# Column sums as rounded parts, a layer norm with a fixed place in the weight stream, and a rotation by transfers

## The chip, the cores and the metric

The kernel runs on one core of a Trainium2 chip. The metric is the device time of one execution in microseconds (us). A core has a matrix engine (TensorE, PE in the profile), a vector engine (VectorE, DVE), a scalar engine with function tables (ScalarE, ACT), a general engine (GpSimd, POOL), a queue engine (SyncE, SP), and DMA engines. Each engine takes its own instructions in a fixed order, and engines wait for each other by semaphores.

## The reference, cut to what matters

Two decoder layers run over 512 prompt tokens and 8 sample tokens (520 columns here), 1024 channels wide:

```python
def hybrid_layer(x, ...):
    h = rms_norm(x, norm_g)
    glu, gate_a, q, k, v, gate_b, mg_a, mg_b = split_in(h @ w_in)
    u = glu[..., :CONV_WIDTH] * sigmoid(glu[..., CONV_WIDTH:])
    c = depthwise_conv31(concat([conv_buf, u])) + conv_b
    c = silu(layer_norm(c, ln_g, ln_b)) * silu(gate_a)
    y_a = c @ w_conv_out
    q, k = partial_rope(q, pos), partial_rope(k, pos)   # 16 of 64 dims: x1*cos - x2*sin, x2*cos + x1*sin
    o = windowed_attention_with_sinks(q, k, v)
    y_b = (o * silu(gate_b)) @ w_attn_out
    return x + (sigmoid(mg_a) * y_a + sigmoid(mg_b) * y_b) @ w_out
```

A final rms_norm follows the second layer. All is float32, to a tolerance that plain bfloat16 products would miss.

## The kernel before, in words

Channels lie on the 128 partitions and tokens run along a row, so an activation of 1024 channels is eight tiles of 128x520. The weights of a layer come as 82 **units** of 1024x128: one DMA from SP brings a unit (`raw`, two buffers), ACT rounds it to fp32r (`whi`, L126), DVE subtracts to get the rest (`wlo`, L127; three buffers each). `Unit.step` (L134) issues three matmuls for each of eight channel tiles and each half of 260 tokens: high times high, low times high, high times low. That is 48 matmuls a unit. Activations are split the same way (`split`: ACT cast L97, DVE subtraction L98). A unit's two result banks (`mm`) are double-buffered, so a unit can't begin until the work that reads the result of the unit two before it is done; the third GLU unit of a layer uses two spare banks, `T` and `V`.

The order in a layer is: GLU 16 units in pairs a and b (i = 0 to 7), K, V, Q 8, gate_b 8, MB and MA 16 (between which stand the attention's scores L506, transposes L532 and values L541), gate_a 8, YB 8, YA 8, OUT 8. Below, gate_a 1 is the first unit of gate_a, and so on. The first three GLU pairs multiply rows that aren't normalized yet; the factor R of the rms norm (`rstd`: ACT Ln and Exp L183 and L186, DVE L184 to L189) is multiplied into their results, and the normalized rows `hh, hl` are made meanwhile (DVE L266, cast L97, subtraction L98) for the fourth pair onward. A scheduler sets the order on each engine, with priorities and `issue_after` ties from the program.

A sum over channels (`Sum`) adds eight tiles on DVE (L165) and then multiplies the float32 total `ssum` with a matrix of ones on PE, one matmul for each half (`total`, L170). This happens for the rms norm of each layer, for the mean and the variance of the convolution's layer norm (L600 on), and at the end. The layer norm then scales eight tiles (L613) on DVE, and YB's units end in `mgb = result * mgb` (L641), which frees the unit's banks. Results of gate_a are copied out by ACT (L620). ACT also makes 24 sigmoids of gate values (L623, L624, L626), tied behind the last Exp of the attention. K's rotation takes the partner rows by two float32 matmuls with a permutation matrix (L348), read out of PSUM by two multiplications (L349).

Of the kernel before, what the change touches and what calls it, by code (L numbers as in the profile page):

```python
# [10 lines left out]
F32R = mybir.dt.float32r  # L11
AF = mybir.ActivationFunctionType
ALU = mybir.AluOpType

D = 1024
# [4 lines left out]
HALF = TOK // 2  # L20
KT = 8
TAPS = 31
PAD = TAPS - 1
HD = 64
# [8 lines left out]
W_GLU, W_K, W_V, W_Q, W_GB, W_MB, W_MA, W_GA, W_YB, W_YA, W_OUT = (  # L33
    0, 16, 17, 18, 26, 34, 42, 50, 58, 66, 74)
# [2 lines left out]
P_G, P_CW, P_CB, P_LG, P_LB, P_SK, P_SS = 0, 8, 256, 264, 272, 280, 296  # L37
N_P = 297

C_ID, C_SW, C_MASK, C_FG = 0, 128, 256, 512  # L40
N_C = 520


@with_exitstack
def hybrid_step(ctx, tc, x_in, w_in, par, const, rope, conv_st, kc_in, vc_in,
                y_out, ncp, nkp, nvp, ncs, nks, nvs):
    nc = tc.nc
# [21 lines left out]
    def g(dt=F32):  # L69
        return gp.tile([128, TOK], dt, tag="g", name=name("g"))  # L70
# [4 lines left out]
    def two(t):  # L75
        return t.rearrange("p (a b) -> p a b", a=2)

    def sbank():
        return psS.tile([128, 512], F32, tag="S", name=name("S"))
# [6 lines left out]

    con = cst.tile([128, N_C], F32, name="con")
    ident = con[:, C_ID:C_ID + 128]
    swap = con[:, C_SW:C_SW + 128]
    ones = cst.tile([128, 128], F32, name="ones")  # L90
    V.memset(ones, 1.0)
    eps = cst.tile([128, 1], F32, name="eps")
    V.memset(eps, EPS)

# [52 lines left out]
    class Sum:  # L147
# [27 lines left out]
        def totals(self):  # L175
            return [self.total(0), self.total(1)]

    def rstd(sums, halves=(0, 1)):
        y0, v, a = tmp("y0", 1), tmp("v", 1), tmp("a", 1)
        c = slice(halves[0] * HALF, (halves[-1] + 1) * HALF)  # L180
        for hf, s in zip(halves, sums):
            h = slice(hf * HALF, (hf + 1) * HALF)
            A.activation(y0[:, h], s, AF.Ln, bias=eps, scale=1.0 / D)  # L183
            V.tensor_scalar(v[:, h], s, 1.0 / D, EPS, op0=ALU.mult, op1=ALU.add)  # L184
        y0, v, a = y0[:, c], v[:, c], a[:, c]
        A.activation(y0, y0, AF.Exp, scale=-0.5)  # L186
        V.scalar_tensor_tensor(a, y0, -0.5, y0, op0=ALU.mult, op1=ALU.mult)
        V.tensor_tensor(v, v, a, op=ALU.mult)
        V.scalar_tensor_tensor(v, v, 1.5, y0, op0=ALU.add, op1=ALU.mult)  # L189
        return v  # L190
# [4 lines left out]
    def square(x):  # L195
        s = tmp("sq", 3)
        A.activation(s, x, AF.Square)
        return s
# [49 lines left out]
        after(rows, xt[i], i)  # L248
    after(squares)
    nc.sync.dma_start(con, const)  # L250
    xres = None

    for l in range(L):
# [20 lines left out]
        for i in range(KT):  # L274
# [6 lines left out]
            if i == 0:  # L281
                for k in range(KT):
                    for u in first:
                        u.step(0, k)
                        u.step(1, k)
                R = rstd(sq.totals())
                a, b = first
            else:
                a = Unit(l, W_GLU + 2 * i, *src, spare=(i == 1))
                a.half(0)  # L290
                a.half(1)
            u = up.tile([128, PAD + TOK], F32, tag="u", name=f"u{l}_{i}")
# [40 lines left out]


        kps = Unit(l, W_K, hh, hl).both()
        kn, kcos, ksin, krot = g(), g(), g(), g()
        nc.gpsimd.dma_start(kcos, rope[2])
        nc.gpsimd.dma_start(ksin, rope[3])
        A.copy(two(kn), kps)
        V.tensor_tensor(krot, kn, kcos, op=ALU.mult)  # L340
        vps = Unit(l, W_V, hh, hl).both()
        vt = g()
        A.copy(two(vt), vps)
        nc.gpsimd.dma_start(nvp[l], vt[:, T - 128:T])
        for hf in range(2):
            c = slice(hf * HALF, (hf + 1) * HALF)
            kss = sbank()
            PE.matmul(kss[:, :HALF], swap, kn[:, c], start=True, stop=True)  # L348
            V.tensor_tensor(ksin[:, c], kss[:, :HALF], ksin[:, c], op=ALU.mult)  # L349
        V.tensor_tensor(krot, krot, ksin, op=ALU.add)  # L350
        nc.gpsimd.dma_start(nkp[l], krot[:, T - 128:T])
        KH, KL = [], []
        for kv in range(2):
# [248 lines left out]
        for i, c in enumerate(cs):  # L602
            sm.add(i, c)
        mu = tmp("a", 1)
        for hf, s in enumerate(sm.totals()):
            A.mul(two(mu)[:, hf, :], s, -1.0 / D)
        sm = Sum()
        for i, c in enumerate(cs):
            V.tensor_tensor(c, c, mu, op=ALU.add)
            sm.add(i, square(c))  # L610
        R2 = rstd(sm.totals())
        for c in cs:
            V.tensor_tensor(c, c, R2, op=ALU.mult)  # L613


        sga = []
        for i in range(KT):
            ps = Unit(l, W_GA + i, hh, hl).both()
            s = g()
            A.copy(two(s), ps)  # L620
            sga.append(s)
            with tc.issue_after(exp_ins[0].ins):
                A.activation(mgb[i], mgb[i], AF.Sigmoid)  # L623
                A.activation(mga[i], mga[i], AF.Sigmoid)  # L624
                sg = tmp("sq", 3)
                A.activation(sg, s, AF.Sigmoid)  # L626
            V.tensor_tensor(s, s, sg, op=ALU.mult)
# [15 lines left out]

        yh, yl = [], []
        for i in range(KT):
            ps = Unit(l, W_YA + i, ch, cl).both()
            V.tensor_tensor(two(mga[i]), ps, two(mga[i]), op=ALU.mult)  # L647
            V.tensor_tensor(mga[i], mga[i], mgb[i], op=ALU.add)
            a, b = split(mga[i], new=og)
            yh.append(a)  # L650
            yl.append(b)
# [93 lines left out]
def _constants():  # L745
# [2 lines left out]
    r = np.arange(128)  # L748
    con[r, C_ID + r] = 1
    d = r % HD  # L750
    partner = np.where(d < 8, r + 8, np.where(d < 16, r - 8, r))
    con[r, C_SW + partner] = 1
    j = np.arange(256)[None, :]
    q = r[:, None]
    ok = np.where(j < 128, j > q, j - 128 <= q)
# [74 lines left out]
```

## Time and profile before

| what | value |
|---|---|
| time, median of 3 runs | 1064.87 us (1064.74 to 1064.91) |
| profiled execution, its own time | 1064.98 us |
| its span, first to last instruction | 1063.2 us |
| mean granted clock of TensorE | 0.997 |
| busy PE, DVE, ACT, POOL | 99%, 80%, 49%, 7% |

The span is 1.8 us shorter than the execution's own time. PE's busy share is that of a pipeline: a matmul is shown with some 284 ns, while the next one starts about 0.12 us after it. So lengths are read from starts: in the second layer's third GLU unit 47 matmuls lie between the starts 541.88 and 547.52 us, 0.12 us each, and a unit takes 5.76 us.

### The profile page before, as it was taken

To read this page: it belongs to the slowest core of one execution; us is meant where nothing else is said; L and a number is where in the kernel's file an instruction comes from. 1 tells how busy PE (TensorE), PEld (TensorE's weight loads), DVE (VectorE), ACT (ScalarE), POOL (GpSimd) and SP (SyncE) were. 2 spreads that over 40 slices of the span, in tenths; PEclk is the share of its full clock that TensorE was granted. 3 is DMA by queue.
4 is the path that set the end of the run, shared out by engine and by line. 5 is a ranking of instruction groups with operands and counts; after the bars stand their busy time and mean duration, and the time that the engine had idled before them with its cause. 6 is when DMAs were issued, how large, how long until landed. Compare 5 with 4: busy or idle time off the path is not lost.

```text
span 1063.2 us, 21526 instructions
## 1 busy us (share of the span) xinstructions
PE 1049.8 (99%) x8742; PEld 1034.9 (97%) x8742; DVE 855.4 (80%) x1572; ACT 516.5 (49%) x953; POOL 79.5 (7%) x180
## 2 busy tenths in 40 slices
PE   8999999999999999999999999999999999999996
PEld 8999999999999999999999999999999999999995
DVE  7999999999999587455569999899999976944545
ACT  7621433356667784224453234434576686822322
POOL 0001211001011000000101013100001000000000
PEclk9999999999999999999999999999999999999998
DMA  7334574332321215233334337633232212252312
GB/s 234 127 120 132 173 237 144 102 117 80 105 90 66 80 60 198 82 100 117 133 100 140 120 113 238 205 119 119 81 112 81 87 60 80 87 178 95 99 61 81
DMA packets 45220, 126.42 MB, mean 119 GB/s; under 512 B 6384, under 2 KB 10048, under 8 KB 45120
## 3 DMA queue, kind: packets, MB, share of 16 engines
q1 hardware_dynamic: 39024, 111.81, 32.0%
q0 software_dynamic: 4800, 12.16, 3.6%
q8 instruction: 68, 1.11, 0.4%
q10 hardware_dynamic: 1296, 1.07, 0.3%
q14 instruction: 32, 0.26, 0.1%
HBM read 107.66 MB, written 17.36 MB: 118 GB/s over the span
## 4 chain that ended last, share of the span: by engine, by line
PE 97%; DVE 1%; DMA 1%; SPq 0%; issue 0%; ACT 0%; DVEq 0%; ACTq 0%
PE mm L134 86%; PE S L506 3%; PE pv L541 3%; PE PT L532 2%; PE T L134 1%; PE S L170 1%; PE V L134 1%; DMA g<-x 1%; DMA raw<-w 0%; DVE g L696 0%; DVE ssum L165 0%; PE S L464 0%; PE pvs L486 0%; SPq L123 0%; PE S L348 0%
## 5 line engine op out<-in xcount | busy, mean ns | idle before, releaser
L134 PE MATMUL mm<-g,whi 128*128 128x260 f32 x4160 | 766.2, 284 | 1.0 <-ACT g L215 1.0
L134 PEld LDWEIGHTS mm<-g,whi 128*128 128x128 f32 x4160 | 644.8, 188 | 2.0 <-ACT g L215 1.2
L134 PE MATMUL mm<-g,wlo 128*128 128x260 f32 x2080 | 588.9, 283 | 0.0
L134 PEld LDWEIGHTS mm<-g,wlo 128*128 128x128 f32 x2080 | 392.0, 188 | 0.1
L595 DVE SCALAR_TENSOR_TENSOR acc<-u,par,acc 128x512 f32<-128x512 f32 x464 | 329.0, 744 | 0.2
L126 ACT CAST whi<-raw 128x1024 fp32r<-128x1024 f32 (+1 forms) x168 | 172.9, 1029 | 205.9 <-PE mm L134 165.1
L127 DVE TENSOR_TENSOR wlo<-raw,whi 128x1024 fp32r<-128x1024 f32 (+1 forms) x168 | 200.8, 1196 | 52.7 <-ACT whi L126 52.4
L134 PE MATMUL mm<-o,whi 128*128 128x260 f32 x992 | 179.3, 282 | 1.0 <-DVE g L685 1.0
L134 PEld LDWEIGHTS mm<-o,whi 128*128 128x128 f32 x992 | 153.1, 188 | 1.5 <-issue 0.8
L134 PE MATMUL mm<-o,wlo 128*128 128x260 f32 x496 | 139.5, 282 | 0.0
L134 PEld LDWEIGHTS mm<-o,wlo 128*128 128x128 f32 x496 | 93.2, 188 | 0.0
L518 ACT ACTIVATE p<-p,sm 128x257 f32<-128x257 f32 (+1 forms) x128 | 60.9, 479 | 18.7 <-DVE sm L512 18.6
L512 DVE CUSTOM_DVE_ANT_0 p<-S,con,nsk 128x256 f32<-128x256 f32 (+1 forms) x128 | 52.8, 447 | 7.9 <-PE PT L532 6.1
L534 ACT COPY pts<-PT 128x256 f32<-128x256 f32 (+1 forms) x64 | 33.7, 526 | 50.2 <-PE PT L532 50.2
L510 POOL COPY p<-nsk 128x2 f32<-128x2 f32 x64 | 26.0, 413 | 342.9 <-PE PT L532 289.0
L647 DVE TENSOR_TENSOR g<-mm,g 128x520 f32<-128x520 f32 x16 | 11.2, 700 | 43.1 <-PE mm L134 43.1
L506 PE MATMUL S<-g,g 128*128 128x256 f32 x256 | 41.6, 283 | 0.0
L445 ACT ACTIVATE g<-mm 128x520 f32<-128x520 f32 x16 | 9.7, 606 | 56.7 <-PE mm L134 56.7
L532 PE MATMUL PT<-con,p 128*128 128x128 f32 x224 | 35.6, 276 | 0.0
L506 PEld LDWEIGHTS S<-g,g 128*128 128x128 f32 x256 | 35.1, 188 | 0.0
L641 DVE TENSOR_TENSOR g<-mm,g 128x520 f32<-128x520 f32 x16 | 11.1, 695 | 28.8 <-PE mm L134 28.8
L522 ACT ACTIVATE p<-p,sm 128x128 f32<-128x128 f32 (+1 forms) x64 | 30.5, 480 | 7.5 <-DVE sm L521 7.3
(168 smaller groups left out, 817.5 us busy)
## 6 DMA issues: line engine op xcount, KB each, us to landing
raw<-w SPq DMA_DIRECT2D x162, 512.0 KB, 3.4
qscr<-g SPq DMA_DIRECT2D x32, 256.0 KB, 4.3
g<-qscr SPq DMA_DIRECT2D x32, 256.0 KB, 3.8
g<-x SPq DMA_DIRECT2D x16, 260.0 KB, 4.9
g<-rope POOLq DMA_DIRECT2D x8, 260.0 KB, 4.6
xres<-g POOLq DMA_DIRECT2D x8, 260.0 KB, 2.3
g<-xres SPq DMA_DIRECT2D x8, 260.0 KB, 4.9
ncs<-g POOLq DMA_DIRECT2D x8, 248.0 KB, 3.1
```

The lines of the kernel that those rows point to most:

```text
L126: mark[2] = A.copy(self.hi[:, ks, :], self.raw[:, ks, :])
L127: mark[0] = V.tensor_tensor(self.lo[:, ks, :], self.raw[:, ks, :], self.hi[:, ks, :].bitcast(F32), op=ALU.subtract)
L134: mark[1] = PE.matmul(self.acc[hf], a[:, k, :], b[k][:, c], start=(k == 0 and j == 0), stop=(k == KT - 1 and j == 2))
L506: PE.matmul(S3[:, kv, :], qs[t, kv][:, b * 128:b * 128 + 128], K[kv][:, k0:k0 + 256], start=(j == 0), stop=(j == 1))
L510: G.tensor_copy(p[:, :, nk:nk + 1], nsk[:, 2 * t:2 * t + 2].unsqueeze(2))
L512: V.tensor_tensor_reduce(out=p[:, kv, :nk], in0=S3[:, kv, :nk], in1=con[:, C_MASK + 256 - nk:C_MASK + 256], op0=ALU.add, op1=ALU.min, scal ...
L518: exp_ins[0] = A.activation(p[:, kv, :nk + 1], p[:, kv, :nk + 1], AF.Exp, bias=nm[:, kv:kv + 1], scale=-1.0, accum_out=dn[:, kv:kv + 1])
L522: A.mul(p[:, 0, :nk], p[:, 0, :nk], dn[:, 0:1])
L532: PE.transpose(PT[:, kv, kb, :], p[:, kv, kb * 128:kb * 128 + 128], ident)
L534: A.copy(pts[t][:, :, j0:j0 + nb, :], PT[:, :, :nb, :])
L541: PE.matmul(pv[kv * 64:kv * 64 + 64, j * 128:(j + nb) * 128], vb[:, j * 128 + kv * 64:j * 128 + kv * 64 + 64], pts[t][:, kv, 2 * j:2 * j + ...
L595: V.scalar_tensor_tensor(dst, us[i][:, k:k + T], cw(i, k), acc[i], op0=ALU.mult, op1=ALU.add)
```

## The change

Five edits. A new `totals_of_parts` splits `ssum` as activations are split (one cast, one subtraction) and multiplies both parts with ones rounded to fp32r: four short matmuls in place of two float32 ones. It serves the mean and the variance of both layers and the second layer's first norm sum. The first layer's norm sum and the final sums stay. The third GLU unit (`second`, banks T and V) is issued ahead of the norm sum. The layer norm's two stages are tied into the loop over gate_a, behind its units 3 and 8, and the units of gate_a and YA are each tied behind the matmul before. K's partner rows are brought by four transfers from POOL's queue into a zeroed tile, and multiplied once.

```diff
--- before.py
+++ after.py
@@ -37,8 +37,8 @@
 P_G, P_CW, P_CB, P_LG, P_LB, P_SK, P_SS = 0, 8, 256, 264, 272, 280, 296
 N_P = 297
 
-C_ID, C_SW, C_MASK, C_FG = 0, 128, 256, 512
-N_C = 520
+C_ID, C_MASK, C_FG = 0, 128, 384
+N_C = 392
 
 
 @with_exitstack
@@ -86,9 +86,9 @@
 
     con = cst.tile([128, N_C], F32, name="con")
     ident = con[:, C_ID:C_ID + 128]
-    swap = con[:, C_SW:C_SW + 128]
     ones = cst.tile([128, 128], F32, name="ones")
     V.memset(ones, 1.0)
+    ones_r = cst.tile([128, 128], F32R, name="onesr")
     eps = cst.tile([128, 1], F32, name="eps")
     V.memset(eps, EPS)
 
@@ -175,6 +175,13 @@
         def totals(self):
             return [self.total(0), self.total(1)]
 
+        def totals_of_parts(self):
+            parts, sums = split(self.acc), [sbank()[:, :HALF] for _ in range(2)]
+            for hf, ps in enumerate(sums):
+                for j, t in enumerate(parts):
+                    PE.matmul(ps, ones_r, two(t)[:, hf, :], start=(j == 0), stop=(j == 1))
+            return sums
+
     def rstd(sums, halves=(0, 1)):
         y0, v, a = tmp("y0", 1), tmp("v", 1), tmp("a", 1)
         c = slice(halves[0] * HALF, (halves[-1] + 1) * HALF)
@@ -248,6 +255,7 @@
         after(rows, xt[i], i)
     after(squares)
     nc.sync.dma_start(con, const)
+    A.copy(ones_r, ones)
     xres = None
 
     for l in range(L):
@@ -283,10 +291,23 @@
                     for u in first:
                         u.step(0, k)
                         u.step(1, k)
-                R = rstd(sq.totals())
+                second = Unit(l, W_GLU + 2, *src, spare=True)
+                second.half(0)
+                for k in range(KT):
+                    second.step(1, k)
+                    if k == 2:
+                        far = mark[1]
+                if l == 0:
+                    with tc.issue_after(far.ins):
+                        sums = sq.totals()
+                else:
+                    sums = sq.totals_of_parts()
+                R = rstd(sums)
                 a, b = first
+            elif i == 1:
+                a = second
             else:
-                a = Unit(l, W_GLU + 2 * i, *src, spare=(i == 1))
+                a = Unit(l, W_GLU + 2 * i, *src)
                 a.half(0)
                 a.half(1)
             u = up.tile([128, PAD + TOK], F32, tag="u", name=f"u{l}_{i}")
@@ -333,21 +354,21 @@
 
 
         kps = Unit(l, W_K, hh, hl).both()
-        kn, kcos, ksin, krot = g(), g(), g(), g()
+        kn, ks, kcos, ksin, krot = g(), g(), g(), g(), g()
+        G.memset(ks, 0.0)
         nc.gpsimd.dma_start(kcos, rope[2])
         nc.gpsimd.dma_start(ksin, rope[3])
         A.copy(two(kn), kps)
+        for r in (0, HD):
+            for d in (0, 8):
+                nc.gpsimd.dma_start(ks[r + d:r + d + 8, :], kn[r + 8 - d:r + 16 - d, :])
         V.tensor_tensor(krot, kn, kcos, op=ALU.mult)
         vps = Unit(l, W_V, hh, hl).both()
         vt = g()
         A.copy(two(vt), vps)
         nc.gpsimd.dma_start(nvp[l], vt[:, T - 128:T])
-        for hf in range(2):
-            c = slice(hf * HALF, (hf + 1) * HALF)
-            kss = sbank()
-            PE.matmul(kss[:, :HALF], swap, kn[:, c], start=True, stop=True)
-            V.tensor_tensor(ksin[:, c], kss[:, :HALF], ksin[:, c], op=ALU.mult)
-        V.tensor_tensor(krot, krot, ksin, op=ALU.add)
+        V.tensor_tensor(ks, ks, ksin, op=ALU.mult)
+        V.tensor_tensor(krot, krot, ks, op=ALU.add)
         nc.gpsimd.dma_start(nkp[l], krot[:, T - 128:T])
         KH, KL = [], []
         for kv in range(2):
@@ -602,20 +623,30 @@
         for i, c in enumerate(cs):
             sm.add(i, c)
         mu = tmp("a", 1)
-        for hf, s in enumerate(sm.totals()):
-            A.mul(two(mu)[:, hf, :], s, -1.0 / D)
-        sm = Sum()
-        for i, c in enumerate(cs):
-            V.tensor_tensor(c, c, mu, op=ALU.add)
-            sm.add(i, square(c))
-        R2 = rstd(sm.totals())
-        for c in cs:
-            V.tensor_tensor(c, c, R2, op=ALU.mult)
+
+        def centre():
+            for hf, s in enumerate(sm.totals_of_parts()):
+                A.mul(two(mu)[:, hf, :], s, -1.0 / D)
+            sq = Sum()
+            for i, c in enumerate(cs):
+                V.tensor_tensor(c, c, mu, op=ALU.add)
+                sq.add(i, square(c))
+            return sq
+
+        def scaled(sq):
+            R = rstd(sq.totals_of_parts())
+            for c in cs:
+                V.tensor_tensor(c, c, R, op=ALU.mult)
 
 
         sga = []
         for i in range(KT):
-            ps = Unit(l, W_GA + i, hh, hl).both()
+            with tc.issue_after(mark[1].ins):
+                ps = Unit(l, W_GA + i, hh, hl).both()
+                if i == 2:
+                    sm = centre()
+                elif i == 7:
+                    scaled(sm)
             s = g()
             A.copy(two(s), ps)
             sga.append(s)
@@ -643,7 +674,8 @@
 
         yh, yl = [], []
         for i in range(KT):
-            ps = Unit(l, W_YA + i, ch, cl).both()
+            with tc.issue_after(mark[1].ins):
+                ps = Unit(l, W_YA + i, ch, cl).both()
             V.tensor_tensor(two(mga[i]), ps, two(mga[i]), op=ALU.mult)
             V.tensor_tensor(mga[i], mga[i], mgb[i], op=ALU.add)
             a, b = split(mga[i], new=og)
```

The numbers of code lines move by 7 to 31 in the changed kernel; below, the old ones are used outside the rows of the change.

**PE at the start of the second layer.** Before, the two matmuls of the norm sum stand ahead of the third GLU unit (T, then V); `mm_6587` is the result of the second unit of pair 0.

```order
L134 MATMUL mm_6587<-g_6567,whi_6582 128x260
L170 MATMUL S_6688<-ssum_6124,ones 128x260
L170 MATMUL S_6690<-ssum_6124,ones 128x260
L134 MATMUL T_6739<-g_6118,whi_6734 128x260
L134 MATMUL T_6739<-g_6118,wlo_6735 128x260
```

In the changed kernel the sum stands behind that whole unit; `mm_6821` is the next one (pair 1's unit b).

```order
L134 MATMUL V_6710<-g_6582,whi_6704 128x260
L182 MATMUL S_6763<-g_6759,onesr 128x260
L182 MATMUL S_6763<-g_6760,onesr 128x260
L182 MATMUL S_6764<-g_6759,onesr 128x260
L182 MATMUL S_6764<-g_6760,onesr 128x260
L134 MATMUL mm_6821<-g_6133,whi_6816 128x260
```

The sum has moved behind 48 matmuls, and two float32 matmuls have become four. In the first layer it moves from behind 20 of the unit's matmuls to behind all 48.

**DVE around the layer norm of the first layer.** Before, `mm_5063` is the result of YB 1; the eight scalings (L613) stand before it with two products of the gated branch (L636).

```order
L189 SCALAR_TENSOR_TENSOR v_4536<-v_4536,y_4535 128x520
L627 TENSOR_TENSOR g_4981<-g_4981,sq_4985 128x520
L613 TENSOR_TENSOR u_0_320<-u_0_320,v_4536 128x520
...
L127 TENSOR_TENSOR wlo_5185<-raw_5183,whi_5184 128x1024
...
L636 TENSOR_TENSOR sq_5050<-sq_5050,g_4609 128x520
L636 TENSOR_TENSOR sq_5113<-sq_5113,g_4671 128x520
L641 TENSOR_TENSOR g_2533<-mm_5063,g_2533 128x520
```

In the changed kernel `mm_5078` is YB 1, `mm_5141` YB 2, `wlo_5263` belongs to YB 4.

```order
L196 SCALAR_TENSOR_TENSOR v_5040<-v_5040,y_5039 128x520
L672 TENSOR_TENSOR g_2536<-mm_5078,g_2536 128x520
L639 TENSOR_TENSOR u_0_378<-u_0_378,v_5040 128x520
...
L639 TENSOR_TENSOR u_7_1180<-u_7_1180,v_5040 128x520
L127 TENSOR_TENSOR wlo_5263<-raw_5261,whi_5262 128x1024
L667 TENSOR_TENSOR sq_5065<-sq_5065,g_4551 128x520
L667 TENSOR_TENSOR sq_5128<-sq_5128,g_4613 128x520
L667 TENSOR_TENSOR sq_5191<-sq_5191,g_4719 128x520
L672 TENSOR_TENSOR g_2744<-mm_5141,g_2744 128x520
```

The release of YB 2's banks now stands behind the eight scalings, a weight split and three products, and the variance's sum that all of it follows stands on PE behind gate_a 8 instead of behind 35 matmuls of gate_a 7.

**ACT at the second layer's burst of sigmoids.** Before, the copy of gate_a 1's result (`mm_10943`) is the fourth row behind the table load.

```order
L518 ACTIVATE p_10518,sm_10520<-p_10518,sm_10519 128x257 x2
L623 ACT_TABLE_LOAD
L623 ACTIVATE g_8916<-g_8916 128x520
L624 ACTIVATE g_9009<-g_9009 128x520
L620 COPY g_10992<-mm_10943 128x520
L623 ACTIVATE g_9124<-g_9124 128x520
```

In the changed kernel (`mm_10904` is the same result) ten more sigmoids, two probability scalings (L543), two sigmoids and a transpose's copy (L555) stand before it.

```order
L654 ACT_TABLE_LOAD
L654 ACTIVATE g_8938<-g_8938 128x520
...
L655 ACTIVATE g_10135<-g_10135 128x520
L543 ACTIVATE p_10487<-p_10487,sm_10489 128x256
L654 ACTIVATE g_10256<-g_10256 128x520
L543 ACTIVATE p_10540<-p_10540,sm_10542 128x256
L655 ACTIVATE g_10357<-g_10357 128x520
L555 COPY pts_10380<-PT_10594 128x2x128
L651 COPY g_10953<-mm_10904 128x520
```

The copy has moved from behind 2 sigmoids to behind 14; in the first layer it stays ahead of them.

## Rows read from the trace of the kernel before

**Rows 1.** The page: busy time, share of the span, instructions.

```profile
PE 1049.8 (99%) x8742; PEld 1034.9 (97%) x8742; DVE 855.4 (80%) x1572; ACT 516.5 (49%) x953; POOL 79.5 (7%) x180
```

**Rows 2.** PE's waits: line waited for, us in total, times, longest.

```profile
PE S L170 <- DVE ssum L165: 1.3, 1, 1.3
...
PE S L172 <- ACT sq L687: 0.6, 1, 0.6
```

**Rows 3.** PE in time, the first layer's mean: start, us, instruction.

```profile
351.34 1.04 PE L170 MATMUL S<-ssum,ones 128*128 128x260 f32 x4
352.34 0.28 PE L134 MATMUL mm<-g,wlo 128*128 128x260 f32 x1
```

**Rows 4.** PE in time, the first layer's partner rows.

```profile
112.48 1.04 PE L348 MATMUL S<-g,con 128*128 128x260 f32 x4
113.48 0.28 PE L134 MATMUL mm<-g,wlo 128*128 128x260 f32 x1
```

**Rows 5.** PE in time, the first layer's norm sum, with the idle time before it.

```profile
18.12 0.28 PE L134 MATMUL T<-g,whi 128*128 128x260 f32 x1
...
20.62 0.28 PE L134 MATMUL T<-g,wlo 128*128 128x260 f32 x1
22.20 1.14 PE L170 MATMUL S<-ssum,ones 128*128 128x260 f32 x4 [1.29 <-DVE ssum L165]
```

**Rows 6.** DVE in time, from R to the eighth low part, first layer.

```profile
25.17 0.69 DVE L187 SCALAR_TENSOR_TENSOR a<-y 128x520 f32<-128x520 f32 x1
...
26.63 0.70 DVE L189 SCALAR_TENSOR_TENSOR v<-v,y 128x520 f32<-128x520 f32 x1
...
47.53 0.69 DVE L307 TENSOR_TENSOR u<-u,g 128x520 f32<-128x520 f32 x1
48.15 0.69 DVE L98 TENSOR_TENSOR g<-sq,g 128x520 fp32r<-128x520 f32 x1
```

**Rows 7.** ACT in time, second layer's start: the rounding behind bank V.

```profile
547.72 1.05 ACT L126 CAST whi<-raw 128x1024 fp32r<-128x1024 f32 x1 [2.91 <-PE V L134]
```

**Rows 8.** ACT in time, first layer's variance.

```profile
384.07 1.28 ACT L183 ACT_TABLE_LOAD   x1
385.37 0.85 ACT L183 ACTIVATE y<-S,eps 128x260 f32<-128x260 f32 x2
386.23 1.28 ACT L186 ACT_TABLE_LOAD   x1
387.52 0.64 ACT L186 ACTIVATE y<-y 128x520 f32<-128x520 f32 x1
```

**Rows 9.** DVE in time, first layer's scalings and the first release of YB.

```profile
392.20 4.97 DVE L613 TENSOR_TENSOR u<-u,v 128x520 f32<-128x520 f32 x8
397.09 1.22 DVE L127 TENSOR_TENSOR wlo<-raw,whi 128x1024 fp32r<-128x1024 f32 x1
...
400.05 0.69 DVE L641 TENSOR_TENSOR g<-mm,g 128x520 f32<-128x520 f32 x1
```

**Rows 10.** PE in time, the start of YB 1 in the first layer.

```profile
391.53 0.28 PE L134 MATMUL mm<-o,whi 128*128 128x260 f32 x1
```

**Rows 11.** ACT in time, the second layer's burst of sigmoids.

```profile
866.08 0.64 ACT L623 ACTIVATE g<-g 128x520 f32<-128x520 f32 x1
...
867.14 0.57 ACT L620 COPY g<-mm 128x520 f32<-128x520 f32 x1
```

**Rows 12.** PE in time there, values and transposes of the attention.

```profile
865.79 1.73 PE L541 MATMUL pv<-pts,g 128*64 128x256 f32 x16
867.46 0.33 PE L532 MATMUL PT<-con,p 128*128 128x128 f32 x1
```

**Rows 13.** DMA issues: KB each, median us from issue to landing.

```profile
qsam<-sq POOLq DMA_DIRECT2D x12, 4.0 KB, 1.9
```

**Rows 14.** ACT and DVE in time, first layer: K's copy and its rotation.

```profile
106.95 0.59 ACT L339 COPY g<-mm 128x520 f32<-128x520 f32 x1 [4.67 <-PE mm L134]
...
113.12 0.87 DVE L349 TENSOR_TENSOR g<-S,g 128x260 f32<-128x260 f32 x2 [0.21 <-PE S L348]
```

More of the change, by code (lines that the diff above doesn't have):

```diff
@@ L750, in _constants @@
     d = r % HD
-    partner = np.where(d < 8, r + 8, np.where(d < 16, r - 8, r))
-    con[r, C_SW + partner] = 1
     j = np.arange(256)[None, :]
```

## The prediction

> **What bounds the kernel now.** The busy shares come first: PE is busy for 1049.8 of 1063.2 us, DVE for 80% [rows 1]. PE's list of waits has five lines that come to 5.0 us, from the 1.3 us before the first layer's norm sum to the 0.6 us of a final sum [rows 2]; the chain that ended last lies on PE for nearly all of its length. So time goes away only if PE gets less to do or one of these waits goes, and any new wait of PE is paid in full. DVE and ACT matter where PE needs their results. That makes two sums: what PE is spared, and how late DVE and ACT are at the places where the change moves a step.
>
> **What PE is spared.** Three terms.
>
> - Float32 sums. From the mean's matmuls at 351.34 to the second matmul behind them at 352.34 pass 1.00 us; without them it would be 0.12, so they cost 0.88 [rows 3]. Four short matmuls of the same width, at the 0.12 us of any other, cost 0.48. Five sums change: 5 x 0.40 = 2.0 us. The trace has no matmul with rounded ones. It can't be cheaper than 0.12, and if each were as long as a float32 one (0.44) nothing but 0.9 us a sum would be lost; I take 0.12, since the operands are as wide and of the type that all units use.
> - Partner rows. The same 1.00 us stands around L348 [rows 4], so 0.88 goes in each layer: 1.8 us. What replaces it is costed below.
> - The wait. T's 20th matmul could have been followed by another at 20.74, but the sum began at 22.20 [rows 5]. With 28 more matmuls ahead of it, the sum would come at 18.12 + 48 x 0.12 = 24.0 with its total long ready. That spares 1.4 us.
>
> Together 5.2 us.
>
> **What comes late instead.** Five places; a unit is 5.76 us, and a matmul 0.12.
>
> (a) *The first layer's normalized rows.* R is now made from a sum at 24.0 instead of 22.20. Ahead of its Ln, ACT rounds a weight unit that needs the buffer of the unit just ended: 24.1 + 0.95, then Ln 0.87 and Exp 0.64 as in [rows 8] (no table loads here), 26.6. DVE first subtracts that unit's low part, to 26.3, and takes the two reads of the sum, to 27.0; its three steps take 27.33 - 25.17 = 2.16 [rows 6], so R is there at 29.2 instead of 27.33. From R to the eighth low part DVE needed 48.84 - 27.33 = 21.5 us without a pause worth naming [rows 6]. One weight split (1.2 us) now lies ahead of R, and the product L307 at 47.53 behind the eighth part, which leaves 19.7, and the part is ready at 48.9. PE reaches it 46 matmuls after its fourth pair begins: 24.0 + 0.88 + 3 x 5.76 = 42.2, plus 46 x 0.12, 47.7. **PE waits 1.2 us.**
>
> (b) *The second layer's.* Here the sum moves behind a whole unit. The rounding that waits for bank V ran at 547.72 [rows 7]; without the 0.88 of the sum ahead of it the unit ends at 546.64 and the rounding begins at 546.84. It stands ahead of Ln now: 547.8, Exp done at 549.3; DVE's split and two reads to 549.6, R at 551.8. The same 19.7 us end at 571.5, and some 0.3 us more are lost because ACT puts a copy that waits for the end of the next unit, a rounding and a table load ahead of the casts and the first sigmoid. PE reaches the eighth part at 546.64 + 0.48 + 17.28 + 5.52 = 569.9. **PE waits 1.9 us.**
>
> (c, d) *YB 4 in both layers.* S is the end of gate_a 8, behind which the variance's sum now stands. ACT: copy 0.5 and rounding 0.95 (1.5), table load 1.30 and Ln 0.86 (3.7), load and a sigmoid 1.95 (5.6), load 1.29 and Exp 0.64: S + 7.6, where the same chain took 4.1 us from load to Exp's end before [rows 8]. DVE: 2.16 for R (9.7), release of YB 1 0.61 (10.3), eight scalings 4.89 (15.2), weight split 1.13 (16.4), three products 1.8 (18.2), release of YB 2 0.7: S + 18.9 [rows 9]. YB 4 needs YB 2's banks, and PE comes to it at S + 0.48 + 3 x 5.76 = 17.8. Before, YB 3 was due at 391.53 + 11.52 = 403.05, and its release ended at 400.74 [rows 9, 10], 2.3 us early. **PE waits 1.1 us a layer, 2.2.**
>
> One rule speaks for a much larger price. The table load and what follows it take 1.30 us: 384.07 to 385.37 [rows 8]. The Trainium skill ("ScalarE: Activation LUTs", section "What ACT_TABLE_LOAD costs") gives 1283 ns for the load and some 1380 ns of draining with every switch, 2.66 us in all; the load agrees with the row, the drain isn't seen in it. By the page the three switches would take 4.1 us more in each layer, an estimate from its figure, and the time would be some 8 us above the sum below.
>
> (e) *gate_a 3 in the second layer.* It needs gate_a 1's banks. The first sigmoid of the burst begins at 866.08 and two take 1.06 [rows 11]: twelve end at 872.4, then two probability scalings 0.8, two sigmoids 1.06, a small copy 0.27, and the copy 0.57: 875.1. PE passes 865.79 with 47 matmuls of gate_a 2 still to come; with the values (1.7), two transposes (0.4) and four more (0.5) that makes 874.0 [rows 12]. **PE waits 1.1 us.** In the first layer the copy stays ahead of the burst: nothing.
>
> The rest is covered. The mean's cast and subtraction come while gate_a 3 runs. K's copy ends at 107.5 and the multiplication stood at 113.12 [rows 14]; small transfers of POOL's queue land 1.9 us after issue [rows 13], which leaves 3.7 us for issuing four. Landing at once would change nothing; at 5 us, DVE would stop for 1 to 2 us, ahead of a weight split that PE wants only some 11 us later. The zeroing and the rounded ones lie in idle time of POOL and ACT.
>
> **The sum.** -5.2 + 1.2 + 1.9 + 2.2 + 1.1 = +1.2 us on the profiled execution's 1064.98 (span 1063.2 and 1.8 around it): 1066.2. That execution is 0.1 above the median, so the median goes to **1066.1 us**, +0.11%. A difference of 0.2%, 2.1 us, is about what a measurement of this kernel can tell from none: 1062.7 and 1067.0 are the limits.
>
> **The rivals.**
>
> *The new waits mostly don't come.* For it: each is a difference of two long sums and only 1 to 2 us wide, and DVE and ACT have idle time elsewhere. If none comes, 1064.87 - 5.2 = 1059.7; if only (b), the widest, stays, 1061.6. Against it: in (a) DVE had just 0.4 us to spare before (48.84 against a need at 22.20 + 0.88 + 28 x 0.12 + 17.28 + 5.52 = 49.2), while PE now comes 1.5 us sooner. Chance 0.20.
>
> *Slower: the casts starve DVE in (a) and (b).* ACT takes instructions in order, and at the start of each layer the copy of a unit's result that isn't finished stands ahead of a rounding (0.95), the casts (0.55 each) and a table load with its sigmoid (1.9). If DVE has to stop for the load as well as for the casts, about 1.2 us a layer, (a) and (b) come to 2.4 and 3.1 and the total to 1068.5. It decides from 0.5 us a layer, where 1067.0 is passed. For it: in the trace the load does stand between casts and sigmoid. Against: DVE has other products in its row meanwhile. Chance 0.30, with what a shifted order of the attention may add.
>
> *The switches cost more where they stand now.* Three of them lie between the variance's sum and R. If each held ACT for a second load's time, 1.28 us [rows 8], YB 4 would wait 3.8 us longer in each layer, 1073.8. That Ln begins 1.30 us after its load does speaks against it: 0.02. (This is what the page's drain would do.)
>
> *The gains are eaten, as summed.* 0.48.
>
> **How the numbers follow.** The likeliest case is the sum, 1066.1, and its own range, with half a microsecond either way on each of the five waits that add as errors do, is 1064.9 to 1067.3. The range of 1061.6 to 1068.5 reaches to the first rival with (b) alone and to the second; beyond it lie about 0.1 on either side. Faster 0.20, same 0.48, slower 0.32.
>
> **What would show it.** In the changed kernel's trace: no wait before the first layer's norm sum; PE waits of 1 to 2 us for a low part (L98) near 48 and 570 us, for YB 2's release near 403 and its fellow of the second layer, for gate_a 1's copy near 874; R ending near 29 and 552 us; the sums at 0.12 us a matmul. The forecast is wrong if R comes sooner, if DVE's 19.7 us shrink, or if the rounded ones cost more.

## The result and the profile after

The changed kernel takes 1070.65 us (1069.68 to 1071.03, five runs) against 1064.81 us for the kernel before on the same chip: 1.0054 times, 95% interval 1.0041 to 1.0068. It is slower, by 5.8 us. Forecast were 1066.1 us and a range that ended at 1068.5. The profiled execution took 1070.6 us, its span is 1068.8.

PE's work has become smaller, its waits have grown. The page's line of busy times answers to [rows 1]:

```profile
PE 1049.1 (98%) x8734; PEld 1033.8 (97%) x8734; DVE 857.9 (80%) x1575; ACT 518.8 (49%) x959; POOL 83.8 (8%) x190
```

PE's list of waits answers to [rows 2] (line waited for: us in total, times, longest):

```profile
PE mm L134 <- DVE g L98: 3.4, 2, 1.7
PE mm L134 <- ACT g L97: 2.8, 2, 1.4
...
PE mm L134 <- ACT g L319: 1.0, 1, 1.0
PE PT L553 <- ACT pts L555: 0.9, 1, 0.9
```

The wait before the first layer's norm sum (1.3 us) is gone. New are two for a low part (L98), two named after the cast L97, one for a copy out of a GLU unit's banks (L319) and one for a copy out of the transpose's bank (L555). L97 is the profile's choice among several releasers: in the row of the first of these waits, PE goes on at 411.41 us, the casts end at 411.30 and the release of YB 2's banks (L672) at 411.26.

Where the time goes can be read by pairing weight matmuls: the n-th of before and the n-th of after do the same work, since the order of units is the same. The start of each unit's first one, after minus before, in us (below, the **lag**; units are counted from 0 through both layers, 82 to a layer, and GLU pairs by their i):

| unit | lag | what lies since the line above |
|---|---|---|
| 4 (GLU pair 2) | -2.04 | no wait for the sum; 0.3 of it lies ahead of the sum, where PE waits less for the first rows at 6 us |
| 8 (GLU pair 4) | +3.01 | first layer's normalized rows |
| 20 (Q) | +2.23 | partner rows by transfers |
| 52 (gate_a 3) | +1.14 | mean of the layer norm comes later, so its sum isn't in yet |
| 60 (YB 3) | +1.16 | both sums of the layer norm |
| 64 | +2.77 | YB 4 |
| 88 (second layer, GLU pair 3) | +2.22 | second layer's start |
| 92 (GLU pair 5) | +4.53 | second layer's normalized rows |
| 132 (gate_a 1) | +3.51 | partner rows, attention |
| 136 | +4.78 | ACT's burst of sigmoids, mean |
| 144 (YB 5) | +5.61 | variance, YB 4 |
| last | +5.59 | end |

The largest step is the second one: 5.05 us between units 4 and 8, where 1.2 was forecast. In PE's order of time there are two waits in it (start, us, instruction, idle time before it and its releaser):

```profile
41.53 0.28 PE L134 MATMUL mm<-g,whi 128*128 128x260 f32 x1
42.81 0.39 PE L134 MATMUL mm<-g,whi 128*128 128x260 f32 x1 [1.01 <-ACT g L319]
...
47.91 0.28 PE L134 MATMUL mm<-g,wlo 128*128 128x260 f32 x1
49.87 0.68 PE L134 MATMUL mm<-g,whi 128*128 128x260 f32 x2 [1.69 <-DVE g L98]
```

From start to start the first costs 1.17 us more than a matmul, the second 1.85. What stands behind the second is no wait. Stretches of that time (busy PE, weight loads PEld, DVE, ACT, POOL, each with its count, then PEclk, the granted clock as a share, DMA share, GB/s):

```profile
47.00:49.00 2.00, 1.14 (x8) 0.73 (x6) 2.00 (x4) 0.82 (x2) 0.10 (x1) 1.00 0.19 30
49.00:51.00 2.00, 1.13 (x6) 1.13 (x6) 2.00 (x5) 0.18 (x1) 0.44 (x1) 0.76 0.91 308
51.00:53.00 2.00, 2.00 (x11) 2.00 (x11) 2.00 (x4) 0.00 (x0) 0.54 (x1) 0.50 0.51 193
53.00:56.00 3.00, 3.00 (x25) 3.00 (x25) 3.00 (x9) 0.57 (x2) 0.00 (x0) 0.92 0.00 0
```

From 51 to 53 us the granted clock is 0.50, which is 1.2 of 2.4 GHz, though PE is busy without a gap: 11 matmuls lie in 2 us, where 17 belong. Sixteen matmuls start 0.215 us apart instead of 0.12, which is 1.5 us. So 1.17 + 1.85 + 1.5, and 0.5 in a few slower starts around the waits, make the 5.05 us.

Why R is late there is in ACT's and DVE's order of time, which answers to [rows 6]:

```profile
26.24 1.05 ACT L126 CAST whi<-raw 128x1024 fp32r<-128x1024 f32 x1 [3.40 <-DMA raw<-w]
27.20 0.84 ACT L190 ACTIVATE y<-S,eps 128x260 f32<-128x260 f32 x2
```

```profile
30.60 0.70 DVE L196 SCALAR_TENSOR_TENSOR v<-v,y 128x520 f32<-128x520 f32 x1
...
49.13 0.69 DVE L98 TENSOR_TENSOR g<-sq,g 128x520 fp32r<-128x520 f32 x1
...
50.07 0.69 DVE L98 TENSOR_TENSOR g<-sq,g 128x520 fp32r<-128x520 f32 x1
```

The rounding ahead of R's Ln waited 3.40 us, and for a transfer, not for the buffer of the third GLU unit. R was there at 31.30 us, not at 29.2, and the eighth low part at 50.76, 19.5 us behind it (19.7 were forecast). PE's wait ends already with the seventh, at 49.82: PE needs that one six matmuls before the eighth.

The wait before, at 42.81, is for a copy that frees a unit's banks. On ACT it stands behind a step of the convolution that waits for a product of DVE, and behind a cast:

```profile
40.89 0.82 ACT L611 ACTIVATE acc<-u,par 128x512 f32<-128x512 f32 x1 [0.62 <-DVE u L328]
41.61 0.61 ACT L97 CAST g<-sq 128x520 fp32r<-128x520 f32 x1
42.12 0.64 ACT L319 COPY g<-mm 128x260 f32<-128x260 f32 x2
```

At the second layer's start the rounding did wait for bank V, as forecast: it began at 549.41 us, R ended at 554.46, the seventh part at 573.74 and the eighth at 574.68, and PE waited 1.85 us until 573.79, for the seventh again. By the lag this start costs 2.3 us.

At YB 4 ACT and DVE did what the sum said, row by row (these answer to [rows 8, 9]):

```profile
392.88 1.05 ACT L126 CAST whi<-raw 128x1024 fp32r<-128x1024 f32 x1
393.95 1.28 ACT L190 ACT_TABLE_LOAD   x1
395.25 0.84 ACT L190 ACTIVATE y<-S,eps 128x260 f32<-128x260 f32 x2
396.11 1.28 ACT L657 ACT_TABLE_LOAD   x1
397.40 0.64 ACT L657 ACTIVATE sq<-g 128x520 f32<-128x520 f32 x1
398.06 1.28 ACT L193 ACT_TABLE_LOAD   x1
399.35 0.64 ACT L193 ACTIVATE y<-y 128x520 f32<-128x520 f32 x1
```

```profile
402.72 4.96 DVE L639 TENSOR_TENSOR u<-u,v 128x520 f32<-128x520 f32 x8
407.60 1.22 DVE L127 TENSOR_TENSOR wlo<-raw,whi 128x1024 fp32r<-128x1024 f32 x1
408.74 1.91 DVE L667 TENSOR_TENSOR sq<-sq,g 128x520 f32<-128x520 f32 x3
410.57 0.69 DVE L672 TENSOR_TENSOR g<-mm,g 128x520 f32<-128x520 f32 x1
```

From gate_a 8's copy at 392.39 to Exp's end are 7.6 us, to the end of YB 2's release 18.9. Three table loads stand between the sum and R, and each next function starts 1.29 to 1.30 us after its load. The Trainium skill ("ScalarE: Activation LUTs", section "What ACT_TABLE_LOAD costs") adds some 1380 ns of draining to the load at each switch; no row here shows it either.

### The profile page after: what moved, and what is told of

The parts are those of the page before. It is cut to its first block, busy times and chain, and to the rows that moved or that the text cites. A ratio compares the mean times of both kernels' runs of the same rounds, so it can differ in the third digit from the quotient of the medians.

```text
span 1068.8 us, 21545 instructions
## 1 busy us (share of the span) xinstructions
PE 1049.1 (98%) x8734; PEld 1033.8 (97%) x8734; DVE 857.9 (80%) x1575; ACT 518.8 (49%) x959; POOL 83.8 (8%) x190
## 4 chain that ended last, share of the span: by engine, by line
PE 87%; DVE 6%; ACT 3%; issue 1%; DMA 1%; SPq 0%; DVEq 0%; ACTq 0%
PE mm L134 78%; PE S L527 3%; PE PT L553 2%; PE pv L562 2%; DVE wlo L127 1%; DVE u L639 1%; DVE sq L274 1%; DMA raw<-w 1%; DVE g L98 1%; PE T L134 1%; DMA g<-x 0%; ACT whi L126 0%; ACT g L97 0%; DVE g L728 0%; ACT g L654 0%
## 5 line engine op out<-in xcount | busy, mean ns | idle before, releaser
L555 ACT COPY pts<-PT 128x256 f32<-128x256 f32 (+1 forms) x64 | 33.7, 526 | 48.3 <-PE PT L553 48.3
L679 DVE TENSOR_TENSOR g<-mm,g 128x520 f32<-128x520 f32 x16 | 11.2, 700 | 42.7 <-PE mm L134 42.7
L97 ACT CAST g<-sq 128x520 fp32r<-128x520 f32 (+1 forms) x44 | 27.2, 623 | 16.4 <-DVE sq L667 10.4
L543 ACT ACTIVATE p<-p,sm 128x128 f32<-128x128 f32 (+1 forms) x64 | 30.4, 479 | 9.0 <-DVE sm L542 9.0
```

Of the source, the lines that this page charges most:

```text
L97: A.copy(hi[:, :n], src)
L543: A.mul(p[:, 0, :nk], p[:, 0, :nk], dn[:, 0:1])
L555: A.copy(pts[t][:, :, j0:j0 + nb, :], PT[:, :, :nb, :])
```

## The experiments

Each was run beside the kernel before on the same chip (three chips in all); the medians stand against its 1064.8 to 1065.0 us. "Mended" below is the changed kernel with the norm sums back ahead of the third GLU unit and the layer norm's second stage one unit earlier.

**Norm sums ahead of the third unit.** The block of `second` goes, the old two lines come back:

```diff
-                second = Unit(l, W_GLU + 2, *src, spare=True)
...
-                R = rstd(sums)
+                R = rstd(sq.totals() if l == 0 else sq.totals_of_parts())
                 a, b = first
-            elif i == 1:
-                a = second
             else:
-                a = Unit(l, W_GLU + 2 * i, *src)
+                a = Unit(l, W_GLU + 2 * i, *src, spare=(i == 1))
```

> The changed kernel with the norm sums put back ahead of the third GLU unit in both layers; all else stays. Theory (the late sum makes R late, and PE waits 1.17 and 1.85 us in the first layer, loses 1.5 us more at a lower clock there, and waits 1.85 us in the second): these 6.4 us go, the old wait of 1.5 us before the first layer's sum comes back: 1070.65 - 4.9 = 1065.8 us. Rival (most of the loss lies in the layer norm and the attention's order): less than 2 us better, above 1068.5.

1065.59 us (1065.29 to 1065.86), 5.1 less than the changed kernel. Both starts are clean: PE's waits there are gone, the old one is back, and the clock doesn't fall.

```profile
PE mm L134 <- ACT g L97: 2.8, 2, 1.4
PE S L170 <- DVE ssum L165: 1.1, 1, 1.1
```

So five of the 5.8 us come from moving the norm sums. This says nothing yet on whether late rows or something else at the start is the way.

**The rounding behind R's Exp.** Pair 2's unit b is loaded as before, its rounding tied behind the Exp (`made`):

```diff
...
-                    b = Unit(l, W_GLU + 2 * i + 1, *src)
+                    b = Unit(l, W_GLU + 2 * i + 1, *src, load=i != 2)
+                    if i == 2:
+                        b.load(slice(0, KT))
+                        with tc.issue_after(made.ins):
+                            b.parts(slice(0, KT))
```

> The changed kernel with one weight rounding (pair 2's unit b) moved on ACT from ahead of R's Ln to behind its Exp, in both layers. Theory (in the first layer that rounding waits for its DMA until 26.2 us and holds R up): R at 29.3 instead of 31.3 us, the first of the two waits goes, the second shrinks to about 1.2, the clock stays up: 3.4 us; in the second layer R comes 1 us sooner: 0.9 us; together 1070.65 - 4.3 = 1066.4 us. Rival (DVE's length behind R or casts behind copies set the end, not R): less than 1 us better, above 1069.6.

1068.25 us (1067.21 to 1069.55), 2.4 better; the rival's 1 us is passed, the forecast of 4.3 isn't reached. In the first layer all went nearly as expected: R ends at 29.55 (29.3 expected), the copy's wait is gone, the low part's is 1.41 us from start to start, the clock of the profiled execution stays up. ACT shows that the transfer now holds the rounding alone:

```profile
24.55 0.92 ACT L190 ACTIVATE y<-S,eps 128x260 f32<-128x260 f32 x2 [1.37 <-PE S L170]
25.50 0.64 ACT L193 ACTIVATE y<-y 128x520 f32<-128x520 f32 x1
26.63 1.05 ACT L126 CAST whi<-raw 128x1024 fp32r<-128x1024 f32 x1 [0.49 <-DMA raw<-w]
```

In the second layer nothing was won (waits of 2.03 and 0.40 us in place of 1.85): the weight split now stands between R's own steps on DVE, at 549.45 us, so R ends 4.8 us behind the start of the sum's last matmul, where it was 4.9. Runs with a mean clock of 0.998 took 1067.2 to 1067.5 us, those with 0.995 to 0.997 1068.3 to 1069.6.

**Three buffers for weights as they land.** `tag="raw", bufs=2` becomes 3, and the pool of activations gets 40 tiles instead of 42.

> The changed kernel with three buffers for weights as they land instead of two (and 40 instead of 42 of the activation tiles, to make room). Theory (in the first layer the rounding ahead of R's Ln waits until 26.2 us for a transfer that can't start before a buffer is free at 22.8): the rounding starts at the end of the third GLU unit, 24.1, R is there at 29.2 instead of 31.3, the first of the two waits goes and the second is 1.2 us: 1070.65 - 3.3 = 1067.3 us with the clock up, 1068.5 where it falls once. Rival (the transfer isn't what holds R): R stays at 31.3, 1070 or more.

1070.39 us: the time didn't move, and the forecast of it failed. The mechanism did hold. The rounding waits for bank V, no longer for a transfer:

```profile
25.76 1.05 ACT L126 CAST whi<-raw 128x1024 fp32r<-128x1024 f32 x1 [0.58 <-PE V L134]
```

The copy's wait is gone, the low part's is 0.90 us, the clock stays up; by the lag of units, 4 to 8 cost 1.26 us instead of 5.05. But the third unit's rounding now stands on ACT ahead of the last of the first rows and waits 2.10 us there for its own transfer, until 15.47 (new waits of PE of 0.6 and 0.95 us near 17 us, and 2 us of lag at unit 4). And the scheduler wrote another order around the attention, with new waits of 0.4 to 1.2 us at 306, 353, 830 and 878 us; whether the third buffer or the fewer tiles made it do so isn't told apart.

**Filling the first wait.** Three float32 matmuls of ones on a bank of the sums, tied behind pair 2's last matmul, with the fourth pair behind them; their result isn't used.

```diff
+                if l == 0 and i == EARLY:
+                    with tc.issue_after(mark[1].ins):
+                        spin = sbank()
+                        for _ in range(3):
+                            last_spin = PE.matmul(spin[:, :128], ones, ones, start=True, stop=True)
+                    with tc.issue_after(last_spin.ins):
+                        a.half(0)
+                        a.half(1)
...
```

> The changed kernel with three float32 matmuls of ones times ones (128 columns, some 0.47 us each by the warm-up's) put into PE's queue where the first layer's first new wait stands (near 41.5 us), the fourth pair tied behind them; their result isn't used. Theory (the lower clock of 50 to 53.5 us comes from two waits, 1.17 and 1.85 us, within 9 us): the wait is filled, the clock stays at its upper level in most runs, 1070.65 - 1.3 = 1069.4 us. Rival (one wait of 1.85 us is enough, as at one place of the kernel with the norm a unit earlier): the same 1.5 us are lost, 1070.6 or more.

1070.25 us (1068.44 to 1071.31): inconclusive for the median, and against the theory in the trace. The three take 0.65 us and leave a wait of 0.3. The clock stayed up at 50 us, behind a wait of 1.85 that stood nearly alone, but in the same execution it was 0.50 from 571.7 us on, behind the second layer's wait of 1.86, which stood alone. One wait of that size can be enough, and isn't always: in the changed kernel's profile the second layer's wait lowered nothing. Over all profiled executions here, from 8 us on and ahead of the final sum, five of PE's twelve waits of 1.85 us or more are followed by a stretch at 0.50, and none of the shorter ones. What decides among the twelve stays open.

**The layer norm's second stage one unit earlier.** `elif i == 7:` becomes `elif i == 6:`.

> The changed kernel with the layer norm's second stage tied behind gate_a 7 instead of 8, which puts the variance's sum 2.4 us (first layer) and 4 us (second) sooner. Theory (YB 4 waits 1.55 us in each layer for banks that DVE frees behind the scalings): both waits go, 1070.65 - 3.1 = 1067.6 us, the rest unchanged. Rival (the wait is for the rounded rows of the gated branch, or moves to another unit): 1069.5 or more.

1067.88 us (1067.66 to 1070.32), 2.8 better, as the theory has it. Both waits under L97 are gone from PE's list; the others stand:

```profile
PE mm L134 <- DVE g L98: 3.4, 2, 1.7
PE mm L134 <- ACT g L319: 1.1, 1, 1.1
```

But the run changed two things: the sum came 1.3 us (first layer) and 4.1 us (second) sooner against YB 1's start, and the gate's sigmoid with its table load no longer stands between Ln and Exp. The run with three buffers tells them apart. Its second stage is tied behind gate_a 8, as in the changed kernel, and the sum even comes 1.7 us later against YB 1; only the sigmoid (L657) was put ahead of Ln there:

```profile
393.97 0.64 ACT L657 ACTIVATE sq<-g 128x520 f32<-128x520 f32 x1
...
395.92 0.85 ACT L190 ACTIVATE y<-S,eps 128x260 f32<-128x260 f32 x2
396.79 1.28 ACT L193 ACT_TABLE_LOAD   x1
398.08 0.64 ACT L193 ACTIVATE y<-y 128x520 f32<-128x520 f32 x1
```

YB 2's release then ends 15.9 us behind the start of the sum's last matmul (18.7 in the changed kernel), and YB 4 waits 0.07 us in the first layer and 0.05 in the second. So with the sum as late as it is, the sigmoid between Ln and Exp makes the whole wait; what the sum's place would do by itself, with the sigmoid left there, no run shows. That PE waits for the release of YB 2's banks and not for the cast that ends within 0.05 us of it isn't told apart; only the release stands in YB 4's way in the program.

**The burst spread.** The sigmoids of merge gates i are tied behind gate_a unit i's copy as well:

```diff
-            A.copy(two(s), ps)
+            out = A.copy(two(s), ps)
-            with tc.issue_after(exp_ins[0].ins):
+            with tc.issue_after(exp_ins[0].ins), tc.issue_after(out.ins):
```

> The changed kernel with the sigmoids of merge gates i tied behind the copy of gate_a unit i on ACT, so that the copies stand ahead of the burst. Theory (PE's 1.09 us near 877 us in the second layer is ACT's burst standing ahead of two copies): that wait goes, 1070.65 - 1.1 = 1069.5 us, if the spread sigmoids don't hold another copy up. Rival (it comes from the attention's own chain): no change, or a wait elsewhere.

1068.76 us (1067.53 to 1069.08). The wait near 877 us is gone from the list (PT behind pts, 0.9), and units 132 to 140 gain 1.2 us on the changed kernel. YB 4's waits are 1.25 instead of 1.55. The profiled executions differ by 1.5 us in all; the other 0.4 of the medians' 1.9 no trace shows.

**Partner rows by transfers alone**, on the kernel before: the change's hunk on `ks`, nothing else.

> The kernel before with the transfers of K's partner rows alone. Theory (two float32 matmuls of 0.44 us go in each layer and nothing waits for the transfers): 1064.81 - 1.8 = 1063.0 us. Rival (DVE stands still for the transfers and gives its lateness on to PE): 1064.8 or more.

1071.09 us (1070.89 to 1072.51), 6.1 slower than before: both theories fell. The transfers hold nobody: by unit 20 the lag is -0.92, the 0.88 that a layer was to gain. But at YB 3 PE waits 2.7 us in each layer, and behind the second of these waits the clock falls to 0.50 (930 to 933 us), some 1.5 us more. With nothing that holds the layer norm in its place, the scheduler put a gate's sigmoid between the variance's two Ln, with a table load on either side:

```profile
383.21 1.28 ACT L182 ACT_TABLE_LOAD   x1
384.50 0.48 ACT L182 ACTIVATE y<-S,eps 128x260 f32<-128x260 f32 x1
385.00 1.28 ACT L625 ACT_TABLE_LOAD   x1
386.29 0.64 ACT L625 ACTIVATE sq<-g 128x520 f32<-128x520 f32 x1
386.95 1.28 ACT L182 ACT_TABLE_LOAD   x1
388.24 0.48 ACT L182 ACTIVATE y<-S,eps 128x260 f32<-128x260 f32 x1
...
390.17 1.28 ACT L185 ACT_TABLE_LOAD   x1
391.46 0.64 ACT L185 ACTIVATE y<-y 128x520 f32<-128x520 f32 x1
```

Two loads from the sum to Exp [rows 8] have become four, Exp ends 8.9 us behind the first load instead of 4.1, and the scalings start at 396.16 instead of 392.20. In none of the kernels with the change's ties do the two Ln stand apart; that the ties are the reason is argued, since no run takes them away alone.

**Mended.** Both: old start, second stage behind gate_a 7; without and with the spread burst.

> The same without the spread of the sigmoids: norm sums ahead of the third GLU unit, layer norm's second stage behind gate_a 7. With the sums ahead, the second layer's burst left only 0.4 us of wait. Theory: 1065.6 - 3.1 (YB 4's two waits) = 1062.5 us. Rival (the earlier variance only moves the wait): 1064.5 or more.

1062.46 us (1062.09 to 1063.51), ratio to before 0.9978 (0.9969 to 0.9986): faster than both kernels.

> The changed kernel with three of its placements mended: norm sums ahead of the third GLU unit as before, the layer norm's second stage behind gate_a 7, the sigmoids spread; parts, partner transfers and ties stay. Theory (the five waits and the lost clock are all that stands against the 3.8 us that PE is spared by the parts and the transfers): 1064.9 - 3.8 = 1061.1 us, 1062 with small waits for the mean. Rival (something of the parts or transfers costs as much as it spares): 1064 or more.

1062.37 us (1062.03 to 1062.71): the same. Its burst leaves the mean alone, but PE waits 0.7 us in each layer, at YB 3. Both are some 1.3 us short of the full 1061.1.

**Partner rows by matmul, on mended.**

> The mended kernel with K's partner rows by matmuls again, as before, all else as mended. Theory (the transfers spare PE 0.88 us a layer and cost nothing once the layer norm is held in its place; the 6 us lost by the transfers alone were the layer norm's order): 1062.46 + 1.75 = 1064.2 us. Rival (the transfers themselves cost time): 1062.5 or less.

1062.62 us (1062.23 to 1062.94): the rival's figure, 0.2 from mended. Yet the transfers don't cost anything themselves. By the lag of units mended gains 0.9 by unit 20 and 0.8 by unit 101, where this kernel gains nothing, and gives it back between units 52 and 56 and between 132 and 136, at the mean, where it loses 0.9 and 1.0 and this kernel loses 0.5 and gains 0.4. The cast of the mean's total stands behind ACT's burst. In the mended kernel (first) it begins at 357.69 us, in this one (second), whose burst starts sooner, 0.8 us before that (1.1 us in the second layer):

```profile
357.69 0.63 ACT L97 CAST g<-ssum 128x520 fp32r<-128x520 f32 x1
```

```profile
356.89 0.63 ACT L98 CAST g<-ssum 128x520 fp32r<-128x520 f32 x1
```

What PE was spared ahead of the mean is lost in front of it.

**Float32 sums, on mended.** `totals_of_parts` becomes `totals` for all.

> The mended kernel with float32 sums throughout, all else as mended. Theory (each of five sums costs PE 0.88 us as float32 and 0.48 as four short matmuls): 1062.46 + 2.0 = 1064.5 us. Rival (the cast and subtraction ahead of the sums, or the rounded ones, eat the difference): within 0.7 us of 1062.5.

1063.55 us (1063.32 to 1063.85): 1.1 slower than mended, between theory (2.0) and rival. In the changed kernel's trace the twenty short matmuls do start 0.12 us apart (2.4 us for all). But between units 52 and 56 mended loses 0.90 us and this kernel 0.80: at the first layer's mean, whose parts need a cast behind the burst, nearly nothing is spared. Between 56 and 60, at the variance, mended gains 0.44 and this kernel nothing. In the second layer mean and variance together bring 0.41 and the norm sum 0.36: each layer norm keeps half of the 0.8 us that its two sums were to spare, and that is the 1.1.

**The first layer's sum behind 33 matmuls**, on mended, with the rest of that unit tied behind the sum:

```diff
...
+                    for k in range(3):
+                        second.step(1, k)
+                    with tc.issue_after(mark[1].ins):
+                        sums = sq.totals()
+                    with tc.issue_after(mark[1].ins):
+                        for k in range(3, KT):
+                            second.step(1, k)
...
```

> The mended kernel (norm sums ahead of the third GLU unit, layer norm's second stage behind gate_a 7) with the first layer's sum put behind exactly 33 of that unit's 48 matmuls, where it should be ready without a wait, and R not later than before. Theory (PE then reaches the eighth low part 1.4 us sooner, and DVE had 0.4 us to spare there): the wait moves, about 1.0 us stands at 48 us: 1062.46 - 0.45 = 1062.0 us. Rival (the 1.45 us are kept): 1061.0 us.

1061.49 us (1061.37 to 1062.14), ratio to before 0.9968 (0.9955 to 0.9980), the fastest measured. The wait before the sum is gone and comes back whole at the seventh low part (1.53 us from start to start, near 46.7):

```profile
PE mm L134 <- DVE g L98: 1.4, 1, 1.4
```

By unit 8 the lag is -0.09, where mended has +0.07: of the 1.45 us at most 0.2 is kept. Its 1.0 us over mended builds up from unit 100 on and is not explained by the edit.

## Why the prediction was wrong

*PE as the bound, waits paid in full.* Right: the lag at the end (5.59 us) is the difference of the two executions (5.6).

*What PE is spared.* Float32 sums: right in size, 0.12 us a matmul. Partner rows: right, 0.9 us in each layer at their place. The wait before the sum: gone, 1.4 as forecast. Of all three the end keeps less, since later waits take from them; the forecast had that for the wait and not for the others.

*(a), the step that failed.* "Ahead of its Ln, ACT rounds a weight unit that needs the buffer of the unit just ended: 24.1 + 0.95." The buffer was free then, the weights weren't there. With two buffers for landing weights, that unit's transfer could be issued only when the split that began at 21.57 had read a buffer, and such a transfer takes 3.4 us in the page's list: 26.2. The trace of the kernel before (first) has the same transfer at nearly the same time as the changed kernel's (second):

```profile
23.30 1.64 SPq L123 DMA_DIRECT2D raw<-w  x2
```

```profile
22.81 1.64 SPq L123 DMA_DIRECT2D raw<-w  x2
```

23.30 + 3.4 is 26.7, and there, before, the rounding began when bank V came free, at 26.70: two waits ended together, and the sum moved only one of them. R came 2.1 us later than summed. Two things followed that the sum didn't hold: ACT's row behind R came late too, with the copy in it that frees a GLU unit's banks, so that PE stood at 41.5 already (1.17), and the clock fell behind the second wait (1.5). Together with the wait itself (1.85 for 1.2) this is 4.5 us for 1.2, 3.3 of the 4.5 us by which the time lies above the forecast. Moving the rounding and adding a buffer each took the copy's wait away and left 1.41 and 0.90 us of the other, so the transfer as the cause of these waits is shown. That the clock follows from them is likely, not shown: behind waits of the same size it often stays up. The sum also took the eighth low part for the one that PE waits for; in both layers it was the seventh.

*(b)* 1.9 forecast, 1.85 measured (2.3 by the lag), with R as far behind the rounding as summed. *(c, d)* 1.1 forecast and 1.55 measured each; the chain of 18.9 us was right, the sigmoid between Ln and Exp with it, on which the wait turns out to hang; PE comes to YB 4 somewhat sooner and starts 0.15 us behind the release. *(e)* 1.1 forecast, 1.09 measured; but PE waited first for the transpose's bank, whose copy stands in the same burst ahead of gate_a 1's.

*The rivals.* That casts starve DVE was put at 1.2 us a layer; DVE stood only for 0.56 us in the second layer's row and worked without a pause in the first. Its time, 1068.5, was nearest, for another reason. That the waits don't come fell, and so did the dearer switches: 1.29 to 1.30 us each.

*The clock* had no place in the sum at all. The trace of before had shown 1.3 us of PE's idle time without a fall. In the rows 0.50 stood behind waits of 1.85 us and more, and with two such waits in the same trace only behind one. The Trainium skill ("TensorE: Matmul & The Clock Gate", section "What's actually happening") says that the lower clock is the default and activity lifts it; the rows agree as far as that goes.

## What to carry to other kernels

When a step moves later, ask of each instruction that now stands ahead of it on its engine not only which buffer it needs, but when its data can land: the last free landing buffer plus the transfer. Where two waits end together in the trace, a change that ends one sooner leaves the other. On an engine at 99%, a wait taken away at one place comes back at the next place where a slower chain hands over; look for that place and its slack (0.4 us here) before counting the gain. And an edit that only shortens work can let a scheduler write a worse order far behind it: hold what matters in place, then measure the edit. And when a run takes a wait away, compare the order on the engines too before naming the cause: one unit earlier also moved a sigmoid.

## What was not expected of the hardware

Waits of PE of 1.9 to 2.7 us were at times, in five of twelve cases, followed by a stretch at 1.2 GHz, though PE had work again: some 1.5 us lost each time (in the changed kernel 16 matmuls at 0.215 us). Runs of one kernel differ by 1 to 2 us with their mean clock: with the rounding behind R's Exp 1067.2 to 1067.5 at 0.998 and 1068.3 to 1069.6 at 0.995 to 0.997. The runs of each kernel whose new waits stayed at 1.55 us or below agreed within 0.9 us, but for one run.
